# Row maxima of two heads brought to rows by one product with the identity instead of two

## The chip, the cores and the metric

The kernel runs on one core of a Trainium2 chip. The metric is the device time of one execution in microseconds (us). A core has a matrix engine (PE, with its weight loads listed apart as PEld), a vector engine (DVE), a scalar engine (ACT), GpSimd (POOL) and a queue of DMA issues (SP). They run side by side and wait for each other by semaphores.

## The reference

A two-layer encoder over 1024 tokens of width 1024. The first layer's mixer runs two groups of eight heads: latent attention with a softmax under a causal mask of 64-token chunks, and stick-breaking attention. The second layer's mixer is chunked band attention with 16 heads and a learned bias. Each mixer is followed by a gated feed-forward block. What the change touches is the softmax of the two attentions of this kind:

```python
s_a = jnp.einsum('bqhd,bkhd->bhqk', q_a[:, t0:kend], k_a[:, :kend]) * scale_a
p_a = jax.nn.softmax(jnp.where(chunk_ok, s_a, -jnp.inf), axis=-1)
...
scores = scores + bias.astype(jnp.float32)[None, None]
p = jax.nn.softmax(jnp.where(valid[None, :, None, None, :], scores, -jnp.inf), axis=-1)
```

A softmax needs the maximum of each row of scores, and the kernel has to get it to where it subtracts it.

## The kernel before

Activations are held transposed, features on the 128 partitions and tokens along the free dimension, in two halves of 512 tokens. A float32 product is made of three products of rounded parts (`mm3`, lines 277 to 282: high by high, high by low, low by high).

Attention works on pairs of heads (e = 0, 1). In `mla_attend` (line 1102) and `band_attend` (line 1185) the scores of a block of 128 keys against up to 512 queries stand with the keys on the partitions: `scores` fills one double bank "z" of PSUM with three products per head in the latent attention (L1120 to L1122) or two per head in the band attention (L1201, and L1202 whose rows 64 to 67 carry the negative maxima of the queries against rows of ones). `weighted` (L831) multiplies the exponentials with the values, one product per head: head 0 writes partitions 0 to 63 and head 1 partitions 64 to 127 of a bank "o". `soft_finish` adds up the denominators with two products (L1088), and DVE makes the quotient (L1092 to L1094).

The row maxima come from a pass ahead of that, `mla_max` (line 1039) and `band_max` (line 1161). With the queries on the partitions it makes the high by high scores once more (L1049 and L1175) and lets DVE reduce each block to a maximum per query (L1051 and L1178), into `m2`. Then `neg_max_rows` (line 1026) turns the 128x4 maxima of each head, four blocks of 128 queries, into four rows: DVE reduces `m2` to `m` (L1030); PE multiplies `m` of each head, 128x4 as the stationary operand, with the identity (L1033), which leaves 4 rows of 128 numbers in partitions 0 to 3 of a bank, head 0's in the first and head 1's in the second bank of one "z"; DVE spreads the four rows into the diagonal blocks of a 4x512 operand, with the sign turned (L1035, one instruction per head, against the constant `negblk` in partitions 0 to 3), and writes them into four rows of the queries' operand (partitions 96 to 99 for the latent attention, 64 to 67 for the band). It is called 24 times: four pairs of heads by two halves, and eight pairs by two halves. The operands of L1033 are plain float32, and each of its products stands in the trace as two weight loads and two matmuls (two passes).

What is in flight beside it: `weave` (line 785) mixes the attention of a pair with the projections of the next pair (L280 to L282, bank "mm"), and `with_max` (line 1209) mixes the next maxima into the attention. The order that this writes down is not final: outside the feed-forward blocks, which are pinned, a scheduler in the framework lists the instructions of each engine by its own costs, so an edit in one place may move neighbours. Inside the feed-forward blocks the order is fixed by hand (L74 in the profile, the wrapper that pins).

Of the kernel before, what the change touches and what calls it, by code (L numbers as in the profile page):

```python
# [10 lines left out]
F32 = mybir.dt.float32  # L11
# [3 lines left out]
AX = mybir.AxisListType  # L15

P = 128
# [139 lines left out]
class Trunk:  # L157
# [47 lines left out]
    def load_consts(self):  # L205
        nc, a, cp = self.nc, self.a, self.cp
        self.g = cp.tile([P, G_N], F32, name="gains")
        nc.sync.dma_start(self.g, a["gains"])
        self.eps = cp.tile([P, 1], F32, name="eps")
        nc.vector.memset(self.eps, 1e-6)  # L210
        self.ones = cp.tile([P, P], F32, name="ones")
        nc.vector.memset(self.ones, 1.0)
        self.ident = cp.tile([P, P], F32, name="ident")
        nc.gpsimd.affine_select(out=self.ident, in_=self.ones, pattern=[[1, P]], compare_op=ALU.is_equal,
                                fill=0.0, base=0, channel_multiplier=-1)
        raw = self.tmp("f")
        nc.gpsimd.affine_select(out=raw[:, 0:P], in_=self.ones, pattern=[[-1, P]], compare_op=ALU.is_ge,
                                fill=0.0, base=0, channel_multiplier=1)
        nc.vector.memset(raw[:, P:2 * P], 1.0)
        nc.vector.memset(raw[:, 2 * P:], 0.0)  # L220
        self.masks = cp.tile([P, HALF], F32R, name="masks")
        nc.vector.tensor_copy(self.masks, raw)
        self.tri, self.carry_ones = self.masks[:, 0:P], self.masks[:, P:2 * P]
        self.zeros = self.masks[:, 2 * P:3 * P]
        self.negblk = cp.tile([4, 4], F32, name="negblk")
        nc.vector.memset(self.negblk, -1.0)
        nc.gpsimd.affine_select(out=self.negblk, in_=self.negblk, pattern=[[1, 4]],
                                compare_op=ALU.is_equal, fill=0.0, base=0, channel_multiplier=-1)
# [797 lines left out]
    def neg_max_rows(self, m2, nh, dsts):  # L1026

        nc = self.nc
        m = self.sp.tile([P, 2, 4], F32, tag="m", name=self.nm("m"))
        nc.vector.reduce_max(m, m2[:, :, :, :nh], axis=AX.X)  # L1030
        mt = self.banks()
        for e in range(2):
            nc.tensor.matmul(mt[0:4, e, 0:P], m[:, e, :], self.ident, start=True, stop=True)  # L1033
        for e in range(2):
            nc.vector.tensor_tensor(dsts[e].rearrange("p (a b) -> p a b", a=4),  # L1035
                                    mt[0:4, e, None, 0:P].to_broadcast([4, 4, P]),
                                    self.negblk[:, :, None].to_broadcast([4, 4, P]), ALU.mult)

    def mla_max(self, hf, proj):
# [449 lines left out]
```

## Time and profile before

| | |
|---|---|
| median of 3 runs | 2609.49 us (2604.78 to 2610.32) |
| the profiled execution | 2615.43 us, span 2613.3 us |
| PE busy | 2521.6 us (96%), 11758 instructions |
| DVE busy | 1911.5 us (73%) |
| ACT, POOL busy | 1169.0 us (45%), 522.9 us (20%) |
| latent attention's 8 calls of `neg_max_rows` | between 428.3 and 604.4 us |
| band attention's 16 calls | between 1407.6 and 1853.6 us |

"Busy" of PE counts each matmul to the end of its way through the array, and matmuls overlap, so 96% is not 96% of PE's peak. The granted clock of PE is given in tenths of full speed for each of 40 slices. The chain of work that ended last is followed back from the last instruction, at each step to what released it; a piece of that chain is what moves the end. In that view a line has the start, the time until the next piece, the engine, the tile and the line, and xN tells of N instructions merged.

### The profile page before, as it was taken

What the parts mean: (1) busy time and instruction counts of PE and PEld (TensorE: products, weight loads), DVE (VectorE), ACT (ScalarE), POOL (GpSimd) and SP (SyncE); (2) the same over time, 40 slices, a digit from 0 to 9 for tenths busy, and PEclk for the clock granted to TensorE, in tenths of its full rate; (3) what the DMA queues carried; (4) which work ended last, traced back from release to release, by engine and by line L of the source; (5) the groups of instructions that cost most, each with busy time, mean ns of one, the idle gap of its engine ahead of it and who ended that gap; (6) DMA issues with size and microseconds to landing.
All of it is one profiled execution on the core that took longest, in us unless ns stands there. A gap on an engine that the chain in (4) does not pass through costs nothing.

```text
span 2613.3 us, 33627 instructions
## 1 busy us (share of the span) xinstructions
PE 2521.6 (96%) x11758; PEld 1941.0 (74%) x11758; DVE 1911.5 (73%) x3072; ACT 1169.0 (45%) x2028; POOL 522.9 (20%) x489
## 2 busy tenths in 40 slices
PE   7999999999999999999999999999999999999997
PEld 6766765557778888888787666676777888888876
DVE  6888887775787666777666777777778766667776
ACT  4677676454454334432253333334444443443324
POOL 3333324663000000000021333335400000000004
PEclk9999998999999999999999999999999999999999
DMA  4221100125434344476642222222552434447661
GB/s 137 61 63 53 53 17 29 35 64 159 163 99 161 110 140 142 149 258 216 206 160 67 73 78 80 73 69 89 172 166 96 162 109 141 145 140 260 213 213 69
DMA packets 179433, 319.70 MB, mean 122 GB/s; under 512 B 20545, under 2 KB 36801, under 8 KB 179265
## 3 DMA queue, kind: packets, MB, share of 16 engines
q1 hardware_dynamic: 179264, 317.56, 36.8%
q8 instruction: 93, 1.52, 0.3%
q14 instruction: 76, 0.61, 0.1%
HBM read 222.58 MB, written 84.41 MB: 117 GB/s over the span
## 4 chain that ended last, share of the span: by engine, by line
PE 68%; DVE 12%; DMA 2%; issue 2%; ACT 2%; SPq 0%; DVEq 0%; ACTq 0%
PE z L74 24%; PE mm L74 12%; PE o L74 6%; PE mm L280 5%; PE mm L281 5%; PE mm L282 5%; PE o L831 3%; DVE u L74 2%; DVE f L1093 2%; PE z L1201 1%; PE z L1175 1%; PE z L1202 1%; DVE u L303 1%; DMA wr<-in_w_down 1%; PE z L1088 1%
## 5 line engine op out<-in xcount | busy, mean ns | idle before, releaser
L74 PE MATMUL z<-u,vh 128*128 128x512 f32 x976 | 304.6, 393 | 7.2 <-DVE u L74 7.2
L74 PE MATMUL z<-u,wh 128*128 128x512 f32 x976 | 302.3, 390 | 6.5 <-DVE u L74 6.5
L280 PE MATMUL mm<-u,wh 128*128 128x512 f32 x720 | 291.7, 405 | 2.4 <-DVE u L710 1.1
L281 PE MATMUL mm<-u,wh 128*128 128x512 f32 x720 | 284.4, 395 | 1.4 <-DVE u L248 1.4
L248 POOL TENSOR_TENSOR wl<-wr,wh 128x512 fp32r<-128x512 f32 (+2 forms) x95 | 123.6, 1308 | 802.4 <-ACT wh L243 733.6
L282 PE MATMUL mm<-u,wl 128*128 128x512 f32 x720 | 283.8, 394 | 0.0
L74 PE MATMUL mm<-u,wh 128*128 128x512 f32 x720 | 224.6, 393 | 3.8 <-ACT wh L74 3.8
L74 PEld LDWEIGHTS z<-u,vh 128*128 128x128 f32 x976 | 184.5, 189 | 48.1 <-ACT u L74 8.8
L74 PEld LDWEIGHTS z<-u,wh 128*128 128x128 f32 x976 | 183.1, 188 | 47.4 <-DVE u L74 9.4
L74 PE MATMUL z<-u,vl 128*128 128x512 f32 x488 | 191.1, 392 | 0.0
L74 PE MATMUL z<-u,wl 128*128 128x512 f32 x488 | 190.0, 389 | 0.0
L280 PEld LDWEIGHTS mm<-u,wh 128*128 128x128 f32 x720 | 135.6, 188 | 62.2 <-issue 33.1
L831 PE MATMUL o<-a,u 128*64 128x512 f32 (+3 forms) x768 | 172.4, 485 | 0.3 <-ACT a L1204 0.3
L74 PEld LDWEIGHTS mm<-u,wh 128*128 128x128 f32 x720 | 135.5, 189 | 34.9 <-ACT wh L74 5.7
L281 PEld LDWEIGHTS mm<-u,wh 128*128 128x128 f32 x720 | 135.8, 189 | 32.5 <-issue 8.3
L282 PEld LDWEIGHTS mm<-u,wl 128*128 128x128 f32 x720 | 135.5, 188 | 32.3 <-issue 3.6
L74 PE MATMUL mm<-u,vh 128*128 128x512 f32 x496 | 152.7, 389 | 0.0
L248 POOL TENSOR_TENSOR u<-wr,u 128x512 fp32r<-128x512 f32 x8 | 10.9, 1373 | 671.7 <-ACT u L243 671.7
L74 PE MATMUL mm<-u,wl 128*128 128x512 f32 x360 | 141.2, 392 | 0.7 <-DVE wl L74 0.5
L1204 ACT ACTIVATE a<-a 128x1024 f32<-128x1024 f32 (+3 forms) x96 | 70.6, 738 | 155.3 <-DVE a L1203 155.0
L1072 POOL TENSOR_TENSOR b<-b,a 128x512 f32<-128x512 f32 (+3 forms) x80 | 110.6, 1382 | 135.8 <-ACT a L1204 117.4
L1203 DVE TENSOR_TENSOR a<-z,bias 128x1024 f32<-128x1024 f32 (+3 forms) x96 | 78.7, 823 | 79.5 <-PE z L1202 65.6
(248 smaller groups left out, 5983.1 us busy)
## 6 DMA issues: line engine op xcount, KB each, us to landing
u<-f_t SPq DMA_DIRECT2D x144, 256.0 KB, 5.2
vr<-in_w_up SPq DMA_DIRECT2D x88, 256.0 KB, 4.4
wr<-in_w_gate SPq DMA_DIRECT2D x88, 256.0 KB, 3.5
f_t<-x SPq DMA_DIRECT2D x72, 256.0 KB, 2.0
wr<-in_w_out SPq DMA_DIRECT2D x64, 256.0 KB, 3.0
f_t<-e SPq DMA_DIRECT2D x54, 256.0 KB, 3.6
ld<-f SPq DMA_DIRECT2D x54, 256.0 KB, 5.2
h<-u SPq DMA_DIRECT2D x48, 256.0 KB, 2.5
```

The source lines that it names most:

```text
L74: return lambda *a, **k: self.tc.keep_in_program_order(f(*a, **k))
L248: self.eng(eng).tensor_tensor(lo, src, hi.bitcast(F32), ALU.subtract)
L280: mm(out, wh, xh, start=first, stop=False, skip_group_check=onto)
L281: mm(out, wh, xl, start=False, stop=False, skip_group_check=onto)
L282: mm(out, wl, xh, start=False, stop=last, skip_group_check=onto)
L303: self.eng(eng).tensor_tensor(acc, acc, sq, ALU.add)
L831: self.nc.tensor.matmul(o[rh, cs], vt[j // 4][:, j % 4, rh], w[:, e, cs], start=first, stop=last)
L1072: self.eng("dve" if dest[2] else "pool").tensor_tensor(st["esum"][:, :, cs], old[:, :, cs], ex[:, :, cs], ALU.add)
L1088: nc.tensor.matmul(den[64 * e:64 * e + 64, :], self.ones[:, 0:64], esum[:, e, :], start=True, stop=True)
L1093: nc.vector.scalar_tensor_tensor(r, t, 2.0, r, ALU.add, ALU.mult)
L1203: nc.vector.tensor_tensor(ex[:, :, cs], z[:, :, cs], tk[:, :, xs], ALU.add)
L1204: nc.scalar.activation(ex[:, :, cs], ex[:, :, cs], AF.Exp)
```

## The change

`neg_max_rows` keeps the maxima in one of two constant tiles `maxes` of 128 x 2 x 32, which are set to zero once at the start and used in turn. DVE's reduction writes head 0's four columns at columns 0 to 3 and head 1's at 32 to 35. One product with the first 36 columns as the stationary operand then leaves head 0's rows in partitions 0 to 3 and head 1's in partitions 32 to 35 of the same bank; the columns in between are zero. The second of DVE's two spreading instructions reads from partition 32 instead of from partition 0 of the next bank. Its other input, `negblk`, stays in partitions 0 to 3.

```diff
+        self.maxes = [cp.tile([P, 2, 32], F32, name=f"maxes{i}") for i in range(2)]
+        for m in self.maxes:
+            nc.vector.memset(m, 0.0)
...
-        m = self.sp.tile([P, 2, 4], F32, tag="m", name=self.nm("m"))
-        nc.vector.reduce_max(m, m2[:, :, :, :nh], axis=AX.X)
+        self.maxes.append(self.maxes.pop(0))
+        m = self.maxes[0]
+        nc.vector.reduce_max(m[:, :, 0:4], m2[:, :, :, :nh], axis=AX.X)
         mt = self.banks()
-        for e in range(2):
-            nc.tensor.matmul(mt[0:4, e, 0:P], m[:, e, :], self.ident, start=True, stop=True)
+        nc.tensor.matmul(mt[0:36, 0, 0:P], m.rearrange("p a b -> p (a b)")[:, 0:36], self.ident, start=True, stop=True)
         for e in range(2):
             nc.vector.tensor_tensor(dsts[e].rearrange("p (a b) -> p a b", a=4),
-                                    mt[0:4, e, None, 0:P].to_broadcast([4, 4, P]),
+                                    mt[32 * e:32 * e + 4, 0, None, 0:P].to_broadcast([4, 4, P]),
                                     self.negblk[:, :, None].to_broadcast([4, 4, P]), ALU.mult)
```

The changed file has four lines more ahead of `neg_max_rows`, so a line Lnnn of before is Lnnn+4 there, and L1033 is L1037, L1035 is L1039. Each engine's list has the same work otherwise, except that the scheduler moved some of PE's matmuls by a few places.

PE in the band attention, at the fourth call for heads of the band attention (at 1490 us in the trace of before; o is the attention's output bank, a the exponentials, mm the next pair's projection). Before:

```order
L1033 MATMUL z_13104<-ident,m_13102 4x128 x2
L1201 MATMUL z_13112<-u_12568,u_12641 128x512
L282 MATMUL mm_13143<-u_11625,wl_13140 128x512
L831 MATMUL o_13037<-a_13070,u_12014 64x128
L1202 MATMUL z_13112<-u_12569,y_12642 128x512
L1201 MATMUL z_13112<-u_12573,u_12647 128x512
L831 MATMUL o_13037<-a_13070,u_12014 64x128
L280 MATMUL mm_13143<-u_11653,wh_13139 128x512
L1202 MATMUL z_13112<-u_12574,u_12648 128x512
L1088 MATMUL z_13167<-b_12995,ones 64x512 x2
```

And now:

```order
L1037 MATMUL z_13085<-ident,maxes_157 36x128
L1205 MATMUL z_13092<-u_12552,u_12625 128x512
L286 MATMUL mm_13123<-u_11613,wl_13120 128x512
L835 MATMUL o_13019<-a_13052,u_12002 64x128 x2
L284 MATMUL mm_13123<-u_11641,wh_13119 128x512
L1206 MATMUL z_13092<-u_12553,y_12626 128x512
L1205 MATMUL z_13092<-u_12557,u_12631 128x512
L285 MATMUL mm_13123<-u_11642,wh_13119 128x512
L1206 MATMUL z_13092<-u_12558,u_12632 128x512
L1092 MATMUL z_13147<-b_12977,ones 64x512 x2
```

The two output products of a block, one per head, stood apart with two score products between them; now they follow each other. In the whole list of PE this happens at seven places, five of this kind in the band attention (128 columns) and two in the latent attention (256 columns): 45 output products stood alone before and 31 do now. One of the latter two, at the fourth call, before:

```order
L1033 MATMUL z_4359<-ident,m_4357 4x128 x2
L281 MATMUL mm_4398<-u_3196,wh_4394 128x512
L282 MATMUL mm_4398<-u_3195,wl_4395 128x512
L831 MATMUL o_4364<-a_4290,u_3599 64x256
L1120 MATMUL z_4368<-u_4008,u_3853 128x512
```

And now:

```order
L1037 MATMUL z_4356<-ident,maxes_157 36x128
L285 MATMUL mm_4394<-u_3200,wh_4390 128x512
L286 MATMUL mm_4394<-u_3199,wl_4391 128x512
L835 MATMUL o_4360<-a_4288,u_3603 64x256 x2
L284 MATMUL mm_4394<-u_3288,wh_4390 128x512
L1124 MATMUL z_4364<-u_4008,u_3855 128x512
```

Head 1's output product, which before came twelve score products later, has moved up to head 0's. Over the whole list of PE the number of times that a 64-column product follows a 128-column one falls from 213 to 208.

DVE's list keeps its order around the calls but for a few neighbours; at the last but one call (at 1820 us) a scaling of a projection (L1139, now L1143) that stood between the reduction and the two spreading instructions now stands behind them. Before:

```order
L1030 TENSOR_REDUCE m_16032<-m_15978 128x8
L1139 SCALAR_TENSOR_TENSOR t_16123<-mm_16067,u_11905 128x512
L1035 TENSOR_TENSOR u_15802<-z_16034,negblk 4x512
L1035 TENSOR_TENSOR u_15807<-z_16034,negblk 4x512
L248 TENSOR_TENSOR u_16126<-t_16123,u_16125 64x512
```

And now:

```order
L1035 TENSOR_REDUCE maxes_158<-m_15978 128x2x4
L1039 TENSOR_TENSOR u_15764<-z_15993,negblk 4x512
L1039 TENSOR_TENSOR u_15769<-z_15993,negblk 4x512
L1143 SCALAR_TENSOR_TENSOR t_16081<-mm_16025,u_11893 128x512
```

The spreading instructions no longer stand behind that scaling.

## Prediction

> **What bounds the kernel now.** I read the page first, for the engine that fills the span and for its clock.
>
> ```profile
> PE 2521.6 (96%) x11758; PEld 1941.0 (74%) x11758; DVE 1911.5 (73%) x3072; ACT 1169.0 (45%) x2028; POOL 522.9 (20%) x489
> PEclk9999998999999999999999999999999999999999
> PE 68%; DVE 12%; DMA 2%; issue 2%; ACT 2%; SPq 0%; DVEq 0%; ACTq 0%
> ```
>
> PE is busy nearly everywhere, its granted clock is at 0.9 or more in 39 of 40 slices, and 68% of the chain that ended last are pieces of PE. So an edit that takes PE time away moves the end wherever the chain runs over PE at that place, and by nothing where it doesn't. The second view is therefore the two lines of the operation itself, the third the chain at its calls.
>
> ```profile
> L1033 PEld LDWEIGHTS z<-ident,m x96: 82/86/87, 428.3 to 1853.6; 128*4 128x4 f32 x96
> L1033 PE MATMUL z<-ident,m x96: 270/273/273, 428.3 to 1853.7; 128*4 128x128 f32 x96
> ```
>
> There are 96 passes: 24 calls, two products each, two passes a product. In the timeline and in the chain, one call in the band attention looks like this:
>
> ```profile
> 1490.41 0.60 PE L1033 MATMUL z<-ident,m 128*4 128x128 f32 x4
> ...
> 1490.48 0.53 PE z L1033 x4
> 1491.01 0.43 PE z L1201
> 1491.44 0.23 PE mm L282
> 1491.68 0.36 PE o L831 x2
> 1492.04 0.43 PE z L1202
> 1492.46 0.24 PE z L1201
> 1492.70 0.36 PE o L831 x2
> 1493.06 0.43 PE mm L280
> ```
>
> The first line is the timeline's, the others are pieces of the chain. Two things are to be seen. The four passes of a call are pieces of PE on the chain. And a matmul of 512 columns that follows a narrow product (L1201 behind L1033, L1202 behind L831) takes 0.43 us instead of 0.23 us, so a narrow product costs 0.20 us beyond its own piece.
>
> The chain runs over L1033 in this way at 22 of the 24 calls. At the first (428 us) and the sixth (550 us) it runs over DVE's spreading instruction instead:
>
> ```profile
> 428.76 0.69 DVE u L1035
> 429.50 0.74 PE z L1120
> ...
> 550.25 0.33 PE z L1033 x2
> 551.21 0.68 DVE u L1035
> 551.91 0.69 DVE c L990
> ```
>
> **The change part by part: the product.** Four passes, each 0.273 us long, span 0.60 us, so they start (0.60 - 0.273) / 3 = 0.109 us apart. Two of four go, which takes off 2 x 0.109 = 0.218 us. What is added is the load of 36 columns instead of 4. The trace has no such load, and two rows bound it: 86 ns for 4 columns above, and for 64 columns the median here:
>
> ```profile
> L831 PEld LDWEIGHTS o<-a,u x768: 132/136/231, 86.9 to 1896.1; 128*64 128x64 f32 x192
> ```
>
> That is 50 ns for 60 columns more, so for 32 more I take 27 ns. It lies open once per call, ahead of the first pass, since the second pass's load (113 ns by this) starts beside the first pass. So a call gives 0.218 - 0.027 = 0.19 us, between 0.17 us (the whole 50 ns open) and 0.22 us (none). On the 22 calls where PE is on the chain that is 4.2 us, from 3.7 to 4.8.
>
> **What the scheduler moved.** At seven places two output products that stood apart are now neighbours. What that is worth is read from pieces of the chain with one product (x2, its two passes) and with both (x4), for 128 and 256 columns:
>
> ```profile
> 1455.42 0.37 PE o L831 x4
> ...
> 499.97 0.57 PE o L831 x2
> 500.55 0.43 PE z L1120
> ...
> 1450.46 0.58 PE o L831 x4
> ```
>
> One product alone takes 0.36 us at 128 columns, both together 0.37 us; at 256 columns 0.57 and 0.58 us. The two write different halves of the partitions and go side by side. So each joining saves a whole product with its 0.20 us behind it: 0.56 us at 128 columns and 0.77 us at 256. Five and two of them make 2.8 + 1.5 = 4.3 us. All seven places lie on stretches where the chain runs over PE. Against that, seven joinings should take seven switches from wide to narrow out of PE's list, and only five are gone, so two new ones stand elsewhere. A switch without its columns costs 0.56 us less what 128 columns cost, and that is 0.77 - 0.56 = 0.21 us: 0.35 us, and 0.7 us for two.
>
> **What it does to DVE.** The reduction writes the same eight numbers per partition. The two memsets lie ahead of a wait of DVE's for ACT, 3.19 us long in the first row below, and cost nothing as long as that wait stands; without it they would cost a few tenths of a microsecond, once. The spreading instructions start when the first product is through, so the first comes 0.03 us later with the longer load. The second reads from partition 32 where the first read from partition 0. The trace has no such pair with 4 rows; the nearest are pairs of like length that read the same partitions (L1035 itself) and different halves (L1002):
>
> ```profile
> 4.71 0.75 DVE L328 SCALAR_TENSOR_TENSOR u<-ld,gains,u 128x512 fp32r<-128x512 f32 x1 [3.19 <-ACT u L327]
> ...
> 1490.83 1.28 DVE L1035 TENSOR_TENSOR u<-z,negblk 4x512 fp32r<-4x512 f32 x2 [0.60 <-PE z L1033]
> ...
> 431.02 1.41 DVE L1002 TENSOR_TENSOR c<-mm,u 64x512 f32<-64x512 f32 x2
> ```
>
> The pair takes 1.28 us in the one case and 1.41 us in the other, so I put the second row block 0.13 us later (bounds 0 and 0.13), with the start 0.16 us. The Trainium skill speaks against the change here: "VectorE: DVE Perf Modes", section "Two Vector instructions with no wait between them", says that an instruction whose input starts in another group of 32 partitions than the last one read from that memory is held until all earlier ones are finished. By that rule the new pair is held where the old one overlapped, and the trace bears it out in that 1.28 is less than twice the 0.68 us of one and 1.41 is not; with the rule the sum is the one below, without it the sixth call loses 0.13 us less.
>
> Behind the second spreading instruction stand DVE's score additions (L1203), and behind its rows the second head's L1202. At the call above, L1202 of head 1 starts at 1493.33 in the timeline, and the rows are written at 1490.83 + 1.28 = 1492.11, so 0.16 us more is covered by 1.2 us:
>
> ```profile
> 1493.33 0.40 PE L1202 MATMUL z<-u,u 68*128 68x512 f32 x1
> ```
>
> It counts only at the sixth call, where the chain goes on in DVE, and 0.03 us at the first: 0.2 us together.
>
> **What is late next.** Behind the band calls PE waits for DVE in each pair of heads:
>
> ```profile
> PE z L1201 <- DVE m L1178: 5.7, 5, 1.1
> PE mm L281 <- DVE wl L248: 4.3, 6, 0.8
> ```
>
> These waits could swallow the gain ahead of them if DVE ran at a pace of its own. The chain through the second kind says otherwise:
>
> ```profile
> 1434.04 0.25 PE z L1202
> ...
> 1436.95 2.83 DVE f L1093
> ...
> 1444.10 2.01 DVE wl L248
> 1446.15 0.39 PE mm L281
> ```
>
> It enters DVE from PE's L1202 a few microseconds behind the call, so when PE gets there earlier, DVE's stretch and the wait behind it move along as they are.
>
> **The sum.** 4.2 + 4.3 - 0.7 - 0.2 = 7.6 us. The profiled execution would come to 2615.4 - 7.6 = 2607.8 us; it lies 5.9 us over the median of the runs shown, 2609.5 us, and the same 7.6 us make that 2601.9, so 2602 us.
>
> **The rivals.**
>
> *The joinings buy nothing.* The joined product may wait for an exponential that was in time at its old, later place, or the filler that it displaced leaves a hole. Then 4.2 - 0.7 - 0.2 = 3.3 us are left: 2606.2 us, within 0.2% of before (5.2 us, about what a measurement of this kernel can tell from no change). For it: the joined product at 256 columns moves ahead of twelve score products. Against it: it reads the same block of exponentials as its neighbour, which the first one had already waited for.
>
> *The waits swallow it all.* If the stretches of DVE behind the calls are set by something that PE does not feed (a weight's landing, ACT's casts), the 1.1 and 0.8 us waits grow by what PE saves, and the time stays 2609.5 us. Against it stands the chain above; for it, that this was read at one of six such waits.
>
> *DVE's normalisation stretches.* L1093, which has both inputs in SBUF, varies more than anything else near the calls:
>
> ```profile
> L1093 DVE SCALAR_TENSOR_TENSOR f<-f,f x24: 678/2303/4129, 462.6 to 1899.4; 128x512 f32<-128x512 f32 x24
> ```
>
> It takes 0.68 us at best and 4.13 us at worst, with a median of 2.30, and at 1436.95 it is on the chain. POOL's additions of the denominators run at the same time:
>
> ```profile
> 1499.14 2.38 POOL L1072 TENSOR_TENSOR b<-a,a 128x1024 f32<-128x1024 f32 x1 [3.05 <-ACT a L1204]
> ...
> 1499.25 2.83 DVE L1093 SCALAR_TENSOR_TENSOR f<-f,f 128x512 f32<-128x512 f32 x1
> ```
>
> Where the moved matmuls shift DVE against POOL, a call may go from 2.3 towards 4.1 us. From seven of 24 going all the way, 7 x 1.83 = 12.8 us, it outweighs the gain by more than 5.2 us and gives 2609.5 + 12.8 - 7.6 = 2614.7 us. The Trainium skill, "SBUF — State Buffer", section "SBUF: two separate sides", has an exclusive lock for such a case, which a DVE operation with two SBUF inputs and GpSimd hold in turn. Against it: both engines are fed by the same scores, so they should move together, and a shift may as well shorten the calls.
>
> *The change does something else.* The one product stands in PE's list 24 times for 48 before, so this one is closed.
>
> **How the numbers follow.** The forecast gets 0.60, the joinings without gain 0.22, the swallowing waits 0.12, the stretched DVE 0.06. The first counts as faster by over 0.2%, the next two as within it, the last as slower. The range starts at the upper bounds, 22 x 0.22 + 4.3 = 9.1 us with no new switches and no cost on DVE, so 2600.4, less 2.4 us, nearly half of the spread of the runs shown (5.5 us): 2598. It ends at the first rival with the low bound of the product, 3.7 - 0.9 = 2.8 us, so 2606.7, plus some 1.8 us of that spread: 2608.5. What is left out above is the last two rivals, 0.18.
>
> **What would show it.** The new product: 48 passes, its load near 113 ns, the passes of a call taking some 0.34 us of the chain instead of 0.53. The joinings: pieces "PE o" x4 of 0.37 us where x2 stood twice, behind every second band call. DVE's pair: 1.41 us instead of 1.28. The waits for L1178 and L248: 1.1 and 0.8 us as before; were they longer by 0.4 to 0.8 us each, the second rival holds. L1093's median near 2.3 us; near 4 the third does. The prediction is wrong if PE's sum of starts shrinks by 7 to 8 us and the span doesn't, or if new waits of PE for L831 or L1202 appear near the calls.

## The result and the profile after

| | before | after |
|---|---|---|
| median of 6 runs | 2608.55 us (2604.51 to 2610.34) | 2629.82 us (2627.94 to 2633.31) |
| ratio, 95% interval | 1 | 1.0086 (1.0073 to 1.0099) |
| the profiled execution | 2615.43 us, span 2613.3 us | 2633.31 us, span 2630.4 us |

The kernel became slower by 21 us, where 7.6 us less had been forecast; the time lies over the forecast range. First, the lines of the page of after that answer to the first three of before:

```profile
PE 2539.2 (97%) x11710; PEld 1937.0 (74%) x11710; DVE 1917.7 (73%) x3074; ACT 1168.7 (44%) x2028; POOL 521.0 (20%) x489
PEclk9999999999999999999999999999999999999999
PE 68%; DVE 12%; issue 2%; ACT 2%; DMA 2%; DVEq 0%; POOL 0%; POOLq 0%; ACTq 0%
```

PE has 48 instructions fewer and is busy for 17.6 us more. The granted clock is not the reason: it is at 0.9 or more in all 40 slices. Next the operation itself, in the groups by line of after:

```profile
L1037 PEld LDWEIGHTS z<-ident,maxes x48: 109/110/113, 424.6 to 1860.6; 128*36 128x36 f32 x48
L1037 PE MATMUL z<-ident,maxes x48: 271/273/300, 424.6 to 1860.7; 128*36 128x128 f32 x48
```

48 passes, and a load of 110 ns. In the chain of after, the call that the prediction took from 1490 us reads:

```profile
1500.36 0.34 PE z L1037 x2
1500.70 0.43 PE z L1205
1501.12 0.24 PE mm L286
1501.36 0.37 PE o L835 x4
1501.73 0.43 PE mm L284
```

The call takes 0.34 us of the chain instead of 0.53, and the two output products are one piece of 0.37 us. DVE's two spreading instructions of this call, in the timeline of after:

```profile
1500.74 1.40 DVE L1039 TENSOR_TENSOR u<-z,negblk 4x512 fp32r<-4x512 f32 x2 [0.62 <-PE z L1037]
```

At this call of the band attention, then, after looks as it was forecast to look. To find the place of the loss, the start of each call's first pass was read from the traces; the calls cut the span into stages:

| stage (us, profiled executions) | before | after | |
|---|---|---|---|
| start to call 1 | 428.3 | 424.6 | -3.7 |
| calls 1 to 8 (latent attention) | 175.9 | 179.8 | +3.8 |
| call 8 to 9 (mostly the first feed-forward block) | 803.4 | 813.2 | +9.8 |
| calls 9 to 24 (band attention) | 445.8 | 442.9 | -2.9 |
| call 24 to the end (mostly the second feed-forward block) | 759.9 | 769.9 | +9.9 |

The first stage varies: in the kernels below that have the same work there it is 423.9 to 428.3 us, so its -3.7 tells nothing. The band stage repeats within 0.5 us. By these two executions nearly 20 us were lost in the two feed-forward blocks, whose order is fixed by hand and where no instruction was touched. The chain there, first of before and then of after, from 906 and 909 us on:

```profile
906.60 5.44 PE o L74 x24
912.04 5.44 PE mm L74 x24
917.48 5.44 PE z L74 x24
```

```profile
909.85 5.55 PE o L74 x24
915.40 5.55 PE mm L74 x24
920.96 5.55 PE z L74 x24
```

Both times PE runs with no wait in it, the same 24 matmuls a piece, and they take 226.7 ns each before and 231.3 ns after. Over both blocks, the matmuls of L74 whose successor starts within 260 ns (5465 of 5552 in before, 5475 in after) start 226.62 ns apart in before and 231.04 in after: 5475 x 4.42 ns = 24.2 us. The two stages grew by 19.7 us only, but the profiled execution of before lies 6.9 us over its median: it took 1563.3 us for both stages, and the eight kernels below whose matmuls start 226.6 to 226.7 ns apart took 1555.6 to 1561.0 us, against 1583.1 us in after. The page's groups show the same as longer matmuls, first before, then after:

```profile
L74 PE MATMUL z<-u,vh 128*128 128x512 f32 x976 | 304.6, 393 | 7.2 <-DVE u L74 7.2
L74 PE MATMUL z<-u,vl 128*128 128x512 f32 x488 | 191.1, 392 | 0.0
```

```profile
L74 PE MATMUL z<-u,vh 128*128 128x512 f32 x976 | 310.2, 399 | 4.1 <-DVE u L74 4.1
L74 PE MATMUL z<-u,vl 128*128 128x512 f32 x488 | 193.6, 397 | 0.0
```

In the latent attention the loss sits between calls 3 and 4, where the interval grew from 23.34 to 28.34 us. The chain of after has this there:

```profile
479.84 1.82 DVE m L1055 x2
481.66 0.03 issue
481.69 4.16 DVE u L1009 x2
485.85 0.03 issue
485.88 1.24 DVE m L1055
487.12 0.14 issue
487.25 1.97 PE z L1092 x4
```

L1009 (L1005 of before) copies 32 rows from one SBUF tile to another. Two of these copies took 4.16 us together, and PE's denominators (L1092) came after them. In the same place of before the copies stood apart, with score reductions between them:

```profile
482.30 1.08 DVE u L1005
483.38 0.03 issue
483.41 0.69 DVE c L1002
484.10 0.03 issue
484.13 1.24 DVE m L1051
485.37 0.04 issue
485.41 0.39 PE z L1120
```

The copy took 1.08 us there. It was the scheduler that moved the reductions ahead and put two copies together; the change names neither line. The part ahead of the prediction tells of moved matmuls of PE and a few neighbours on DVE; at this place (479 to 486 us in before) the lists of DVE, ACT and POOL changed as well.

### The profile page after: what moved, and what is told of

Read it like the earlier page. It is cut to its first block, busy times and chain, and to the rows that moved or that the text cites. A ratio compares the mean times of both kernels' runs of the same rounds, so it can differ in the third digit from the quotient of the medians.

```text
span 2630.4 us, 33537 instructions
## 1 busy us (share of the span) xinstructions
PE 2539.2 (97%) x11710; PEld 1937.0 (74%) x11710; DVE 1917.7 (73%) x3074; ACT 1168.7 (44%) x2028; POOL 521.0 (20%) x489
## 4 chain that ended last, share of the span: by engine, by line
PE 68%; DVE 12%; issue 2%; ACT 2%; DMA 2%; DVEq 0%; POOL 0%; POOLq 0%; ACTq 0%
PE z L74 24%; PE mm L74 12%; PE o L74 6%; PE mm L284 5%; PE mm L285 5%; PE mm L286 5%; PE o L835 3%; DVE u L74 2%; DVE f L1097 2%; PE z L1205 1%; PE z L1179 1%; PE z L1206 1%; DVE u L307 1%; DVE u L252 1%; PE z L1092 1%
## 5 line engine op out<-in xcount | busy, mean ns | idle before, releaser
L74 PE MATMUL z<-u,vh 128*128 128x512 f32 x976 | 310.2, 399 | 4.1 <-DVE u L74 4.1
L74 PE MATMUL z<-u,wh 128*128 128x512 f32 x976 | 304.6, 392 | 6.0 <-DVE u L74 6.0
L252 POOL TENSOR_TENSOR wl<-wr,wh 128x512 fp32r<-128x512 f32 (+2 forms) x95 | 122.3, 1294 | 822.8 <-ACT wh L247 751.3
L74 PE MATMUL mm<-u,wh 128*128 128x512 f32 x720 | 225.6, 394 | 3.8 <-ACT wh L74 3.8
L74 PEld LDWEIGHTS z<-u,vh 128*128 128x128 f32 x976 | 185.1, 190 | 49.1 <-ACT u L74 5.7
L74 PEld LDWEIGHTS z<-u,wh 128*128 128x128 f32 x976 | 183.1, 188 | 50.0 <-DVE u L74 8.6
L74 PE MATMUL z<-u,vl 128*128 128x512 f32 x488 | 193.6, 397 | 0.0
L74 PE MATMUL z<-u,wl 128*128 128x512 f32 x488 | 192.3, 394 | 1.0 <-DVE wl L74 1.0
L74 PEld LDWEIGHTS mm<-u,wh 128*128 128x128 f32 x720 | 135.5, 189 | 36.5 <-ACT wh L74 5.7
L74 PE MATMUL mm<-u,vh 128*128 128x512 f32 x496 | 156.0, 396 | 0.0
L252 POOL TENSOR_TENSOR u<-wr,u 128x512 fp32r<-128x512 f32 x8 | 10.9, 1374 | 682.2 <-ACT u L247 682.2
L74 PE MATMUL mm<-u,wl 128*128 128x512 f32 x360 | 142.4, 396 | 0.7 <-DVE wl L74 0.5
```

The source lines that it names most:

```text
L74: return lambda *a, **k: self.tc.keep_in_program_order(f(*a, **k))
L252: self.eng(eng).tensor_tensor(lo, src, hi.bitcast(F32), ALU.subtract)
```

## The experiments

### Where the tiles lie in SBUF

The theory: the feed-forward blocks slowed because the change moved tiles. The two `maxes` take 2 x 256 bytes per partition in the constants, which lie ahead of everything, and the small pool loses the tile `m` (128 bytes with its buffers). So the tiles in front of the small pool (u, and the weights wr, wh, wl) moved up by 512 bytes, and those behind it (e, vr, vh, s, vl, x) by 384. Before, vh stood at 200576 and u at 44416, and the distance 156160 is 305 x 512. After, they are at 200960 and 44928, and the distance leaves 384 when divided by 512. The rival: the new order of the instructions ahead of the blocks, or the new constant itself, changes what the blocks run into.

After with the distance restored by a pad of 128 bytes in the small pool:

```diff
+        self.pad = self.sp.tile([P, 32], F32, tag="pad", bufs=1, name="pad")
+        nc.vector.memset(self.pad, 0.0)
```

> The changed kernel with 128 bytes per partition of padding (and its memset) in the small pool, where the four m tiles stood, so that the phase's tiles lie as far from the heap's tiles as before, modulo 512 bytes; instructions and their order are those of the changed kernel. Theory A (the loss of 2 x 9.9 us in the two feed-forward blocks comes from where the phase's tiles vh, vl, e lie against the heap's tiles u): a 512-column matmul of the feed-forward blocks starts every 226.7 ns again instead of 231.3, and the median falls by about 20 us from the changed kernel's 2629.8 to 2606 to 2610 us. Theory C (the loss is the product's or the order's own): 2628 to 2632 us.

Measured: 2610.85 us, 0.85 us over what theory A expected; ratio to before 1.0012 (1.0003 to 1.0020), and the feed-forward stages came back to 799.9 and 758.4 us. The order of the instructions is that of after but for the one memset. So by the medians 19 of the 21 us are the place of the tiles, and what is left of the change is a loss of 0.1%.

Before, with nothing but a pad of 384 bytes in the small pool:

```diff
+        self.pad = self.sp.tile([P, 96], F32, tag="pad", bufs=1, name="pad")
+        nc.vector.memset(self.pad, 0.0)
```

> The kernel before with 384 bytes per partition of padding in the small pool and nothing else, so that the phase's tiles lie 384 bytes further from the heap's tiles, as in the changed kernel modulo 512. Theory A: both feed-forward blocks lose some 10 us, 2625 to 2631 us. Theory C: 2606 to 2611 us, as before.

Measured: 2630.56 us, 1.0089 (1.0075 to 1.0103). The kernel before is made as slow as after by a tile that nobody reads. Its chain in the first block:

```profile
905.76 5.55 PE o L74 x24
911.32 5.55 PE mm L74 x24
916.87 5.55 PE z L74 x24
```

The same 384 bytes in the constants, where they move the tiles in front of the small pool as well as those behind it:

```diff
+        self.pad = cp.tile([P, 96], F32, name="pad")
+        nc.vector.memset(self.pad, 0.0)
```

> The kernel before with the same 384 bytes ahead of all pools but the constants, so that heap, weights and phase tiles all move by 384 bytes and keep their distances, and the phase's tiles stand at the same place modulo 512 as in the changed kernel. Theory A in its form of distances: 2606 to 2611 us, 226.7 ns per matmul. Theory B (the place of the phase's tiles itself counts, not the distance): 2625 to 2631 us. Theory C: 2606 to 2611 us.

Measured: 2607.37 us, 1.0000 (0.9991 to 1.0008). In this kernel vh lies at 200960, to the byte where it lies in the one above and in after, but u has moved with it. The chain:

```profile
903.61 5.44 PE o L74 x24
909.05 5.44 PE mm L74 x24
914.49 5.44 PE z L74 x24
```

So it is how the tiles behind the small pool lie against those in front of it that costs, not the place of vh alone. For the rule behind it, three more pads in the small pool of before, of 256, 128 and 64 bytes (the diff is that of the 384 bytes with 64, 32 or 16 for 96):

> The kernel before with 256 bytes of padding in the small pool: the distance between phase tiles and heap tiles is 256 modulo 512. Theory A: a loss in the feed-forward blocks, of the same size as with 384 (some 20 us) if any distance other than a multiple of 512 is bad, or none if only odd multiples of 128 are. Theory C: 2606 to 2611 us.

> The kernel before with 128 bytes of padding in the small pool: the distance of phase tiles and heap tiles is 128 modulo 512. If odd multiples of 128 are bad and 256 is not: a loss as with 384, 2625 to 2631 us. If only 384 is bad: 2606 to 2611 us.

> The kernel before with 64 bytes per partition more in the small pool, so the stationary tiles of the feed-forward blocks lie 64 bytes past a multiple of 512 from the moving ones. If any distance that is not a multiple of 256 costs, it takes 2630 us as with 128 and 384 bytes (226.6 to 231.0 ns from matmul to matmul). If 128 and 384 bytes are special, it stays at 2608. Something between, say 2619 us and 228.8 ns, if the cost grows with the distance from the nearest multiple of 256.

All the kernels of this kind together, with the start-to-start time of the matmuls of L74 as defined above:

| kernel | vh less u, left over by 512 | start to start, ns | median us | ratio (95%) |
|---|---|---|---|---|
| before | 0 | 226.62 | 2608.55 | 1 |
| after | 384 | 231.04 | 2629.82 | 1.0086 (1.0073 to 1.0099) |
| after, pad 128 | 0 | 226.65 | 2610.85 | 1.0012 (1.0003 to 1.0020) |
| before, pad 384 | 384 | 231.03 | 2630.56 | 1.0089 (1.0075 to 1.0103) |
| before, 384 in the constants | 0 | 226.63 | 2607.37 | 1.0000 (0.9991 to 1.0008) |
| before, pad 256 | 256 | 226.65 | 2608.40 | 1.0004 (0.9995 to 1.0013) |
| before, pad 128 | 128 | 231.06 | 2630.17 | 1.0081 (1.0068 to 1.0094) |
| before, pad 64 | 64 | 230.68 | 2627.35 | 1.0071 (1.0058 to 1.0083) |

Distances of 0 and 256 are free, and 64, 128 and 384 cost nearly the same. That falls in with the expectation that any distance that is not a multiple of 256 costs, and against one that grows evenly with the way to the next multiple: 64 bytes cost as good as 128. For the feed-forward blocks the rival, order or constant, has fallen: before with a pad has neither.

### The band attention alone

One product in the band attention only; the latent attention calls the old function with two, and its order is that of before. The tile `m` stays, so the distance is 0.

```diff
-        self.neg_max_rows(m2, hf + 1, [qs[e][hf][0][96:100, :] for e in range(2)])
+        self.two_products(m2, hf + 1, [qs[e][hf][0][96:100, :] for e in range(2)])
```

> The one product for the band attention's 16 calls alone; the latent attention keeps its two products and its order of before, and the m tiles that it keeps restore the distance between phase tiles and heap tiles (a multiple of 512 bytes). Theory (the latent attention's loss of 5 to 7 us comes from the order that the scheduler made there): the band's stretch between its first and last call takes 443 us as in the changed kernel instead of 445.8, the latent attention's 174 to 176 us instead of 180 to 183, and the median is 2603 to 2606 us. Rival (the longer stretch in the latent attention is not its order but something that comes with the constant tiles): 2608 to 2612 us, and 180 us there.

Measured: 2605.34 us, 0.9986 (0.9978 to 0.9995). The latent attention's stage is back at 175.9 us, against 182.6 us in after with its pad, and the band's stage keeps its gain with 443.1 us. So the change is a gain in the one mixer and a loss in the other.

### The copy that was moved

The theory for the latent attention's loss: DVE's copies (L1005) stand still while POOL works, and where the scheduler put them in after, POOL works without a break. The rival: PE waits there because the new product's rows or the moved output products come late, whatever the copies take. The timeline of after with its pad (two lines more ahead, so L1011 is the copy) at that place:

```profile
478.99 1.83 POOL L1078 TENSOR_TENSOR b<-a,a 128x768 f32<-128x768 f32 x1 [0.55 <-ACT a L1129]
480.79 2.70 POOL L254 TENSOR_TENSOR u<-c,u 64x512 fp32r<-64x512 f32 x2
480.84 4.15 DVE L1011 CAST u<-u 32x512 fp32r<-32x512 f32 x2
483.45 1.26 POOL L1078 TENSOR_TENSOR b<-b,a 128x512 f32<-128x512 f32 x1
```

POOL runs from 478.99 to 484.71 us without a gap. The two copies begin at 480.84 and end at 484.99. One by one they take 1.52 and 2.71 us, and each ends 0.28 to 0.29 us after an instruction of POOL has ended (at 482.07 and 484.71). The shortest of the sixteen copies, from the groups of before, takes 0.42 us; the one copy in before beside which POOL does nothing at all (at 478.97) is of that length:

```profile
L1005 DVE CAST u<-u x16: 418/968/2578, 416.9 to 555.8; 32x512 fp32r<-32x512 f32 x16
```

The test puts the copy on ACT, in after with its pad and in before:

```diff
-                nc.vector.tensor_copy(lo[64:96, :], self.kc[hf][0:32, :])
+                nc.scalar.copy(lo[64:96, :], self.kc[hf][0:32, :])
```

> The changed kernel with the padding of 128 bytes, and with the 32-row copy of the rotary keys (L1005 of before) put on ACT instead of DVE. Theory D (between the third and fourth call, 5 us are lost because two such copies on DVE wait until POOL, which runs back to back there, lets go of SBUF): the stretch from the third to the fourth call falls from 28.5 to 23 to 24 us, and the median to 2603 to 2607 us. Rival (the stretch is longer for another reason of the order, such as the joined output products): it stays at 27 us or more.

Measured: 2603.02 us, 0.9975 (0.9964 to 0.9986). The interval of calls 3 to 4 went from 28.55 to 22.80 us. The copies on ACT, in the groups of this kernel:

```profile
L1011 ACT CAST u<-u x16: 616/617/619, 412.8 to 551.9; 32x512 fp32r<-32x512 f32 x16
```

They take 617 ns at every place, where DVE's took between 418 and 2578. With the copies gone from DVE, PE's wait of 2.5 us at L1094 for DVE's reduction is gone from the list of waits of the latent attention. This list of the padded after has it as its second line, and that of the kernel with the copy on ACT does not have it:

```profile
PE z L1039 <- DVE maxes L1037: 2.6, 1, 2.6
PE z L1094 <- DVE m L1057: 2.5, 1, 2.5
```

```profile
PE z L1126 <- DVE m L1057: 3.3, 2, 2.4
PE z L1126 <- DVE f L1098: 2.9, 2, 1.7
PE mm L287 <- DVE u L254: 1.2, 1, 1.2
```

The rival's joined output products fall: they stand behind calls 4 and 7, outside this stretch, and are still joined in this kernel. But with the copies on ACT the scheduler also ordered PE's and DVE's work around them anew (between 473 and 483 us, among other places), so the gain is that of the copies and of this order together. That POOL is what the copies stood still for rests on the times above.

What the copy is worth by itself, in before:

> The kernel before with that copy put on ACT and nothing else, to stand beside the last one. Theory D: little to gain, since in the order of before the copies met POOL less: third to fourth call 23 us, 2604 to 2609 us. The difference between the two is then the change without its loss at that place: 1 to 5 us in favour of the one product.

> The kernel before with only the copy on ACT, once more, beside the one above on the same chip: 2602 us (ratio 0.9978). The difference to the run above is the band's one product alone: 2 to 3 us if it is worth what the band's stage shows, 0 if it is swallowed later.

Measured: 2602.08 us, 0.9978 (0.9969 to 0.9986), and in a second measurement, where 2602 was expected, 2604.66 us, 0.9985 (0.9976 to 0.9993). Both expectations of the first measurement missed: before gained more from the copy than the 2604 to 2609 us expected, and the one product, at 2603.02 us with the same copy, is 0.9 us behind it and not 1 to 5 us ahead. The latent attention's stage is 173.0 us in both, 2.9 us less than before. Half of that is the interval of calls 4 to 5, 28.6 us in the profiled execution of before and 27.1 here. It tells nothing: with 384 bytes in the constants or 128 in the small pool, where the order is that of before, it is 27.1 us as well, with 256 or 64 bytes 28.6 or 28.7. What holds is the interval of calls 1 to 2, 19.5 us in all the kernels with the copy on ACT and 20.0 to 20.7 in all without, and that of calls 3 to 4, 23.3 to 22.7 us.

With the copy on ACT the latent attention's stage takes 174.6 us with one product and 173.0 us with two, and the difference is that same varying interval (28.7 and 27.1 us). So in the latent attention no gain of the one product shows even when the copies are out of the way.

### Both gains together

One product in the band attention, two in the latent attention, the copy on ACT:

> One product in the band attention alone, two in the latent attention, with the copy of 32 rows on ACT. If the band's gain (445.8 to 443.1 us) and the copy's (0.22%, 5.7 us) are independent, both come: some 2608.5 - 2.8 - 5.7 = 2600.0 us, ratio 0.9967, and the interval lies under 0.9978. If what one gains ahead is swallowed by a wait that the other leaves, it stays at the copy's alone, 2602 to 2603 us, as it did for the change in both attentions with the same copy (2603.0). Stage by stage: calls 1 to 8 at 173.0 us as with the copy alone, the band at 443.1 us.

Measured: 2600.93 us, 0.9969 (0.9958 to 0.9980), the lowest median of all, 2.0 to 4.2 parts in a thousand under before where the change was 8.6 over it. The interval reaches a little over the 0.9978 that was expected as its bound. The stages are near what was expected, 173.0 us and 443.4 us. The distance to the kernel with the copy alone, measured beside it, is 2604.66 - 2600.93 = 3.7 us, and by the band's stage 2.5 us; the two intervals of the ratio overlap (0.9958 to 0.9980 and 0.9976 to 0.9993), so the sign of the band's gain rests on the stage and on the kernel with the band alone more than on this pair.

## Why the prediction was wrong

**The sum was made of the wrong list.** The step that failed is "The sum. 4.2 + 4.3 - 0.7 - 0.2 = 7.6 us": it holds only what instructions do. Of `maxes` it priced the two memsets, and of `m` nothing, and the tiles' bytes were not asked after. By medians they cost 19.0 us (after against after with its pad); the start times of the matmuls in the feed-forward blocks give 24.2 us, in a profiled execution that lies 3.5 us over its median. No rival named it, so the range of 2598 to 2608.5 us was drawn around four terms while the largest one was missing. The kernels of before with a pad show that term alone: 64, 128 and 384 bytes in the small pool cost 0.7 to 0.9%, 256 there or 384 in the constants nothing.

**The product** was sized rightly where PE bounds: 48 passes, a load of 110 ns (forecast 113), 0.34 us of the chain. Five intervals between calls of the band attention, with no joining in them, were 26.46 to 26.48 us long and are 26.28 to 26.31 us long now, 0.16 to 0.20 us less each, where 0.19 was forecast. From call 22 to 23 nothing came (21.79 to 21.81 us). In the latent attention the interval from call 2 to 3 shows it as well (26.38 to 26.19 us). Those from calls 1 and 6 were not to give anything, by the forecast, and didn't (20.71 to 20.68 and 22.23 to 22.36 us). From call 5 to 6 only 0.06 us are left (22.83 to 22.77); the trace shows no wait of PE for another engine there, and where the rest went is open.

**DVE's pair** was forecast at 1.41 us, from the pair of L1002, and measured 1.40. The two starts lie 713 ns apart in after and 608 in before, where one of the instructions takes 685 and 678 ns, so now the second starts only when the first is through. The Trainium skill, "VectorE: DVE Perf Modes", section "Two Vector instructions with no wait between them", holds an instruction that starts to read in another group of 32 partitions until all earlier ones have finished, and the trace agrees with the rule.

**The joinings** were priced rightly and paid only in part. In the interval from call 12 to 13, PE's time in output products falls from 5.87 to 5.51 us, that of the score products behind them by 0.23 us, and that is the 0.56 us of the forecast and a little more. But the interval falls by 0.57 us (35.83 to 35.26), where the joining and the product were to give 0.75. The waits of the band attention, after, have the rest:

```profile
PE z L1205 <- DVE m L1182: 5.7, 5, 1.1
PE mm L285 <- DVE wl L252: 5.6, 6, 1.0
```

The first is as it was, 1.1 us each, and the forecast that both would stay held for it. The second grew from 0.8 to 1.0 us, 1.3 us over its six places. "DVE's stretch and the wait behind it move along as they are" was true of one path into that stretch and not of all of it. So the rival of the swallowing waits was right for 0.2 of the 0.94 us that two calls, one of them with a joining, were to give.

**The new switches** show in two places. From call 10 to 11 the interval grew from 35.48 to 35.85 us although it lost 0.19 to the product: 0.37 + 0.19 = 0.56 us, of which 0.23 us is that same wait (0.49 to 0.72 us); the 0.33 us left over are near the forecast of 0.35 for a switch, and output products alone take 0.25 us more. From call 23 to 24 it grew by 0.96 us (33.09 to 34.06), in a stretch that the scheduler wrote anew, with other waits of PE for DVE; what of that is a switch wasn't separated. The band as a whole gained 2.9 us of the 5.1 that the forecast had for it (16 x 0.19 + 5 x 0.56 - 0.7).

**The latent attention** was to gain its part of the product, 6 x 0.19 = 1.1 us, and two joinings of 0.77 us. It lost 3.8 us, or 5.4 without the varying interval of calls 4 to 5, and 5.0 of that is the interval of the copies. Its order was read at PE only; that DVE's copies moved behind the reductions was not followed. One of its two joinings lies in the varying interval of calls 4 to 5 and can't be read. The other lies behind call 7, and there the waits took all of it, as the second rival had it. PE reaches the output products of the full 512 columns 8.35 us behind the call's first pass instead of 9.17, which is 0.82 of the 0.96 us forecast for the product and the joining. Then it waits for DVE's additions of the denominators, where it did not wait before, and the interval grows from 31.78 to 32.28 us. First before, then after:

```profile
580.12 1.37 DVE L248 TENSOR_TENSOR u<-ld,u 128x512 fp32r<-128x512 f32 x1 [0.33 <-ACT u L243]
583.79 1.03 PE L1088 MATMUL z<-b,ones 128*64 128x512 f32 x4
```

```profile
579.35 3.02 DVE L252 TENSOR_TENSOR u<-ld,u 128x512 fp32r<-128x512 f32 x1
583.92 1.08 PE L1092 MATMUL z<-b,ones 128*64 128x512 f32 x4 [1.07 <-DVE b L1076]
```

An instruction of DVE ahead of the additions, with two inputs in SBUF like L1093, took 3.02 us instead of 1.37, beside two instructions of POOL that follow each other without a gap until 581.82 us. "All seven places lie on stretches where the chain runs over PE" was read from before and no longer held here.

**DVE's normalisation**, the rival that ended on the other side, did not stretch. The line in after:

```profile
L1097 DVE SCALAR_TENSOR_TENSOR f<-f,f x24: 680/2302/4117, 458.8 to 1905.9; 128x512 f32<-128x512 f32 x24
```

Its median is 2302 ns against 2303. But what it named, DVE standing still while POOL works, is what the traces show at the latent attention's loss, at other instructions: at the copies (5 us) and at L252 behind call 7. The Trainium skill, "SBUF — State Buffer", section "SBUF: two separate sides", names two kinds of DVE operation that hold this lock against GpSimd: those with two SBUF inputs, and those in a mode that uses two ports. The prediction looked for the first kind alone; a plain copy between SBUF tiles stood still here as well, 4.15 us for two beside 0.42 us for one at best. That each of the two ended 0.28 to 0.29 us behind the end of an instruction of POOL agrees with a lock for a whole instruction.

## What to carry to other kernels

A tile that is added or dropped moves all tiles behind it, so the addresses belong to the change as much as the instructions do: compare them, and if a stage slows in which nothing was edited, give the bytes back with a pad before looking for a cause in the order. When a scheduler lists the instructions, read what it moved on every engine that the chain runs over, not only on the one that was edited, and look for SBUF copies that come to stand beside POOL's work. A gain on PE counts up to the next wait for DVE only, so a change that helps one stage can be kept out of the other one.

## What the runs showed of the hardware

The rate of the 128x128 by 128x512 matmuls in the feed-forward blocks depends on how the tiles behind the small pool lie against those in front of it: 226.6 to 226.7 ns from start to start when the distance in a partition is 0 or 256 bytes past a multiple of 512, and 230.7 to 231.1 ns at 64, 128 and 384 bytes, so 2% of PE's rate for a pad that holds nothing. Why is open. With 128 bytes of pad, matmuls on vh followed by others on vh went from 226.9 to 233.8 ns, but those on wh followed by others on wh, which lie at distance 0 from u in all these kernels, went from 226.9 to 230.6 as well.

The order of the products shows why wh is slow too. They alternate between runs of 12 (or 9) matmuls on the w tiles (wh and wl) and runs on the v tiles (vh and vl). With 128 bytes of pad, the full runs of v are slow throughout, 233.0 ns on the mean against 226.7 before. In the full runs of w the first seven matmuls, behind a run of v, start 231.1 ns apart on the mean, the eighth to eleventh 226.7 to 226.8 as before, and the twelfth, ahead of the next run of v, 232.4. The two long runs of 171 matmuls on w alone keep their rate (227.5 and 227.3 ns, against 227.5 and 227.4 before). So in these runs the matmuls on w are slow only next to those on v, which are the ones with a moved operand. Nor is it DVE, ACT or POOL working at the same time: the matmuls in the full runs of v beside which none of the three runs an instruction start 232.1 ns apart with that pad and 226.6 before. DMA beside them wasn't separated. Distances under 64 bytes, and other operand types, weren't tried.
